# One seven-product chunk in each SwiGLU of a two-layer encoder, the third, with all four of its pairs

## The chip, the cores and the metric

The kernel runs on one core of a Trainium2 chip. The metric is device microseconds of one execution of the whole program. The page of the profile tells of one profiled execution; its engines are PE (matrix products), DVE (element-wise work on two tensors), ACT (copies, Silu, Exp), POOL, and SP, which issues nearly all of the DMAs.

## The reference

Two layers work on 256 rows (tokens) of 1024 numbers, all in float32. Each layer adds half a SwiGLU, then a mixer, then half a SwiGLU:

```python
def swiglu(h, w_gate, w_up, w_down):
    return (jax.nn.silu(h @ w_gate) * (h @ w_up)) @ w_down

for layer in range(DEPTH):
    x = x + 0.5 * swiglu(rms_norm(x, ffn1_norm[layer]), ...)
    x = x + mixer(rms_norm(x, mix_norm[layer]))      # attention; even and odd layers differ
    x = x + 0.5 * swiglu(rms_norm(x, ffn2_norm[layer]), ...)
return rms_norm(x, final_norm)
```

`w_gate` and `w_up` are 1024 x 2816, `w_down` is 2816 x 1024. The mixers are not touched by the change.

## The kernel before

**Stages.** The program is six stages, numbered `now.n`: SwiGLU 0, mixer 1, SwiGLU 2, SwiGLU 3, mixer 4, SwiGLU 5. All weights are read once from HBM, mostly 1 MB at a time, into three buffers called `raw`.

**One product.** Each float32 number is split into a high and a low part, and each product of a 128-row block of activations with a piece of weights of 128 x 512 is three matmuls (`mm`, L469 to L471: high by high, high by low, low by high). "Product" below means these three. For the weights, ACT copies the high part (`hi`, L477) and DVE subtracts it for the low part (`lo`, L480). A `Split` is one such step, of 1024 columns (two pieces) or 512 (one); seven tiles of the kind "wp" hold its results. With every product the function `tick` lets one step of the other tasks be recorded, and new splits are recorded at the rate of the tables `RATE`, `AHEAD_RATE`, `SEVEN_RATE`, if a tile is free (`room`). The order of recording is the order on each engine: every engine's queue is in order, written out by hand.

**A SwiGLU.** The 2816 columns of gate and up are worked off as five chunks of 512 (chunk 0 to 4) and a last one of 256. In a plain chunk two row tiles (`tt` 0 and 1) times eight blocks of the contraction make 16 products for the gate and 16 for up. ACT then takes Silu of the gate (L670), DVE multiplies it with up out of PSUM (`glu`, L675), and the result is turned over by two ACT copies (L554, L558) with a DMA transpose between. The down projection takes 11 pairs of 128-row blocks.

**Seven products for eight.** A pair of contraction blocks of two row tiles, gate and up, is a 2 x 2 by 2 x 2 product, and can be had with seven products (Strassen's scheme in Winograd's form). The table `SEVEN` says which chunks do it and for how many of their four pairs; `DOWN` says it for the down projection, by `s` for seven products and `p` for the plain eight. It costs sums: `strassen` makes from one raw tile the sum `two` and two sums in place (`b12`, `b11`, both in `raw`), and four splits, one of 512 columns and three of 1024. The last two are of the kind "sum" and have three tiles of their own (`shi`, `slo`). `x_sums` makes four sums of the activations (K) ahead of the chunk; `SEVEN_WAIT` and `SEVEN_GAP` say after how many products it starts and how far apart its steps stand. At the end of a chunk of seven, `copy` (ACT, L765), `common`, `first_gate` and `rest` (DVE, L773 to L814) put the seven sums together.

**PSUM.** There are eight banks of 512 columns: two called `pj`, three `s`, one `o`, two `tp`. A plain chunk has its gates in `s` and its ups in `pj`. A chunk of seven has the product sums "00", "01", "10" in `s`, "1" and "5" in `pj`, "7" in `tp`. If one or more of its pairs are plain, these come first and need "11" in `o` too, and "6" lies in `tp`; without a plain pair "6" lies in `o`. After the last plain pair, the chunk waits in the program for the tasks of the chunk before (`finish`), and "1" and "5" take the two `pj` banks over. The plain chunk after a chunk of seven has its first gate in `pj` again, by the table `tags`.

Of the kernel before, what the change touches and what calls it, by code (L numbers as in the profile page):

```python
# [20 lines left out]
NT = 2  # L21
# [12 lines left out]


DOWN = {
# [4 lines left out]
}  # L41

SILUS = {0: 3, 2: 3, 3: 3, 5: 3}
# [39 lines left out]

SEVEN = {
    0: {2: 3},
    2: {1: 3, 3: 2},
    3: {1: 2, 3: 2},
    5: {2: 3},  # L90
}
AHEAD_RATE = {
    0: 0.81,
    2: 0.62,
# [6 lines left out]
    3: 1.2,  # L101
    5: 1.08,
}
SEVEN_WAIT = {
    0: 22,
    2: 4,
    3: 5,
    5: 6,
}
SEVEN_GAP = {  # L110
    0: 2,
    2: 4,
# [93 lines left out]
class Trunk:  # L206
# [88 lines left out]
    def plan(self):  # L295
# [16 lines left out]
        def ffn(n, l, stage):  # L312
            c0 = 0
            for ci, w in enumerate(FF_CHUNKS):
                first = stage == 0 and c0 == 0
                if ci in SEVEN[stage]:
                    for k in range(0, KD, 2):
                        pieces = []
                        for i, name in enumerate(("_w_gate", "_w_up")):
                            src = a[n + name][l][k * P : (k + 2) * P, c0 : c0 + w].rearrange("(k p) n -> p k n", p=P)  # L320
                            pieces.append(((slice(0, P), slice(0, 2), slice(i * w, i * w + w)), src))
                        yield pieces, 2, D, [2], "strassen" if k >= KD - 2 * SEVEN[stage][ci] else "wide"
                    c0 += w
# [28 lines left out]
        def odd():  # L352
# [4 lines left out]
            for g in range(2):  # L357
                for nh in range(2):
                    src = w_out[g * 512 : g * 512 + 512, nh * 512 : nh * 512 + 512].rearrange("(j p) n -> p j n", p=P)
                    yield [(slice(0, P), src)], 4, 512, [2], "narrow"  # L360

        yield from ffn("ffn1", 0, 0)
        yield from even()
        yield from ffn("ffn2", 0, 2)
        yield from ffn("ffn1", 1, 3)
        yield from odd()
        yield from ffn("ffn2", 1, 5)
# [24 lines left out]
    def strassen(self, raw, halves):  # L392


        add = lambda o, x, y: self.nc.vector.tensor_tensor(o, x, y, op=ALU.add)  # L395
        first, second = halves(raw[:, 0, :]), halves(raw[:, 1, :])
        b21, b22, b11, b12 = (t[:, i, :] for t in (first, second) for i in range(2))
        flat = raw.rearrange("p k n -> p (k n)")

        def all_sums():  # L400
            two = splits[2].raw = self.t([P, 2, 512], "two")
            add(two, second[:, 1:2, :].to_broadcast([P, 2, 512]), halves(flat[:, 512:1536]))
            add(b12, two[:, 1, :], b22)
            add(b11, b12, b21)


        splits = [
            Split(second[:, 0:1, :], [1], then=all_sums),
            Split(first, [1]),
            Split(first, [1], kind="sum"),  # L410
            Split(second, [1], True, kind="sum"),
        ]
        return splits
# [243 lines left out]
    def ffn(self):  # L657
# [10 lines left out]
        def silu(tt, w, g, s):  # L668
            yield 1
            nc.scalar.activation(s[:, :w], g[:, :w], AF.Silu, scale=self.rstd_of(tt))  # L670

        def glu(tt, f0, w, u, s):
            yield 1
            m = self.t([P, 512], "glu", 3)
            nc.vector.scalar_tensor_tensor(m[:, :w], u[:, :w], self.now.r[tt], s[:, :w], op0=ALU.mult, op1=ALU.mult)  # L675
            self.spawn(transposed(tt, f0, w, m), GLU_WAIT)
# [44 lines left out]
        K = []  # L721
        sevens = SEVEN[self.now.n]
        most = max(sevens.values())

        def x_sums():

            yield SEVEN_WAIT[self.now.n]
            gap = SEVEN_GAP[self.now.n]
            X = []
            for tt in range(NT):  # L730
                while len(self.now.hT[tt]) < KD:
                    yield 1
                x = self.t([P, 2, 512], ("shi", "slo")[tt], FIT["sum"], F32R).bitcast(F32)
                X.append(x.rearrange("p a (k t) -> p (a k) t", t=P)[:, : 2 * most, :])
                hi, lo = (t.bitcast(F32)[:, KD - 2 * most :, :] for t in self.hts[self.now.n, tt])
                nc.vector.tensor_tensor(X[tt], hi, lo, op=ALU.add)
                yield gap
            k0, k1, k2, k3 = (X[tt][:, i::2, :] for tt in range(NT) for i in range(2))
            for o, x, y, op in [
                (k2, k3, k2, ALU.subtract), (k3, k3, k1, ALU.subtract), (k1, k2, k1, ALU.subtract), (k0, k1, k0, ALU.add)  # L740
            ]:
                nc.vector.tensor_tensor(o, x, y, op=op)
                yield gap

            places = [(f"g0_{sum(FF_CHUNKS[:ci]) // P}_", FF_CHUNKS[ci] // P) for ci in range(max(sevens), len(FF_CHUNKS))]
            places += [(f"k{f}", 4) for f in sorted(paired, reverse=True)]
            for (tag, n), k in zip(places, (k0, k1, k2, k3)):
                hi, lo = (self.t([P, n, P], tag + p, 1, F32R)[:, :most, :] for p in "hl")
                self.high_part(hi, k)
                yield gap  # L750
                self.low_part(lo, k, hi)
                K.append([(hi[:, q, :], lo[:, q, :]) for q in range(most)])

        def seven_gates(f0, w, pairs7):

# [96 lines left out]

        f0 = 0
        self.spawn(x_sums())
        for ci, w in enumerate(FF_CHUNKS):
            if ci in sevens:
                seven_gates(f0, w, sevens[ci])
                f0 += w // P
                continue
            self.rate = (AHEAD_RATE if ci + 1 in sevens else RATE)[self.now.n]  # L860

            tags = ["pj", "s", "s", "pj"] if ci - 1 in sevens else ["s", "s", "pj", "pj"]
            G = self.take(KD)
            S = []
            if self.now.n + ci == 0:
                both = self.first_gates(G)
            for tt in range(NT):
                g = both[tt] if self.now.n + ci == 0 else self.project(self.ready(tt), G, tags[tt])
                S.append(self.t([P, 512], "silu", SILUS[self.now.n]))
                self.start(silu(tt, w, g, S[tt]))  # L870
            U = self.take(KD)
            for tt in range(NT):
                u = self.project(self.now.hT[tt], U, tags[NT + tt])
                tasks.append(self.start(glu(tt, f0, w, u, S[tt])))
            f0 += w // P

        w, V = FF_MIXED, self.take(KD)
        for tt in range(NT):
            both = self.project(self.now.hT[tt], V, "s")
            s = self.t([P, 512], "silu", SILUS[self.now.n])  # L880
# [686 lines left out]
```

## Time and profile before

| what | value |
|---|---|
| median of 3 runs | 942.53 us (942.22 to 944.11) |
| the profiled execution | 944.79 us, of which 943.0 us are its span |
| PE busy | 922.9 us, 98% |
| DVE busy | 788.4 us, 84% |
| ACT busy | 679.1 us, 72% |
| POOL busy | 91.6 us, 10% |
| DMA | 183.16 MB, mean 194 GB/s |
| chain that ended last | PE 66%, DVE 16%, ACT 7%, DMA 5% |

Read it so: PE is hardly ever idle, so its waits are few and can be listed one by one. The busy share of PE counts the modelled, overlapping lives of matmuls; the time from one start to the next tells the real pace. A wait is put down to the instruction that ended it. In the rows of a view by stretch, (x..) counts instructions and PEclk is the granted share of the TensorE clock.

### The profile page before, as it was taken

To read this page: it belongs to the slowest core of one execution; us is meant where nothing else is said; L and a number is where in the kernel's file an instruction comes from. 1 tells how busy PE (TensorE), PEld (TensorE's weight loads), DVE (VectorE), ACT (ScalarE), POOL (GpSimd) and SP (SyncE) were. 2 spreads that over 40 slices of the span, in tenths; PEclk is the share of its full clock that TensorE was granted. 3 is DMA by queue.
4 is the path that set the end of the run, shared out by engine and by line. 5 is a ranking of instruction groups with operands and counts; after the bars stand their busy time and mean duration, and the time that the engine had idled before them with its cause. 6 is when DMAs were issued, how large, how long until landed. Compare 5 with 4: busy or idle time off the path is not lost.

```text
span 943.0 us, 12407 instructions
## 1 busy us (share of the span) xinstructions
PE 922.9 (98%) x4399; PEld 753.5 (80%) x4399; DVE 788.4 (84%) x1228; ACT 679.1 (72%) x1091; POOL 91.6 (10%) x152
## 2 busy tenths in 40 slices
PE   8999999999999999999999999999999999999997
PEld 6887888877778788888888878778878788878886
DVE  6799679778869988888978887989777787988897
ACT  7687876477787777875657778657877577769753
POOL 1300000064410000000100000008030000000001
PEclk9999999999999999999999999999999999999999
DMA  8867875554326687776466777575433458488661
GB/s 286 276 183 245 250 212 213 185 151 100 108 91 200 220 215 227 234 231 236 151 181 224 197 232 229 195 257 171 146 125 134 134 167 257 126 271 254 185 223 45
DMA packets 129344, 183.16 MB, mean 194 GB/s; under 512 B 50689, under 2 KB 63745, under 8 KB 129281
## 3 DMA queue, kind: packets, MB, share of 16 engines
q1 hardware_dynamic: 128704, 181.58, 61.4%
q10 hardware_dynamic: 576, 0.79, 0.2%
q8 instruction: 34, 0.56, 0.2%
q14 instruction: 30, 0.24, 0.1%
HBM read 169.76 MB, written 1.05 MB: 181 GB/s over the span
## 4 chain that ended last, share of the span: by engine, by line
PE 66%; DVE 16%; ACT 7%; DMA 5%; issue 4%; SPq 0%; POOL 0%; POOLq 0%; ACTq 0%; DVEq 0%
PE s L470 9%; PE s L471 9%; PE s L469 9%; PE pj L469 9%; PE pj L470 9%; PE pj L471 9%; DVE lo L480 7%; ACT hi L477 2%; DMA glu<-turned 2%; PE o L1039 2%; DVE raw L395 1%; DVE two L395 1%; PE tp L1118 1%; PE o L469 1%; PE o L470 1%
## 5 line engine op out<-in xcount | busy, mean ns | idle before, releaser
L480 DVE TENSOR_TENSOR lo<-raw,hi 128x1024 fp32r<-128x1024 f32 (+1 forms) x372 | 375.5, 1029 | 80.9 <-ACT hi L477 79.5
L477 ACT ACTIVATE hi<-raw 128x1024 fp32r<-128x1024 f32 (+1 forms) x372 | 319.6, 889 | 57.1 <-PE pj L471 16.5
L470 PE MATMUL s<-lo,th 128*128 128x512 f32 x373 | 145.6, 390 | 2.5 <-DVE lo L480 2.5
L469 PE MATMUL pj<-hi,th 128*128 128x512 f32 x367 | 146.6, 400 | 1.3 <-ACT glu L765 1.3
L469 PE MATMUL s<-hi,th 128*128 128x512 f32 x373 | 146.2, 392 | 0.4 <-ACT hi L477 0.4
L471 PE MATMUL s<-hi,tl 128*128 128x512 f32 x373 | 145.4, 390 | 0.0
L470 PE MATMUL pj<-lo,th 128*128 128x512 f32 x367 | 143.5, 391 | 1.7 <-DVE lo L480 1.6
L471 PE MATMUL pj<-hi,tl 128*128 128x512 f32 x367 | 143.3, 390 | 0.0
L470 PEld LDWEIGHTS s<-lo,th 128*128 128x128 f32 x373 | 70.0, 188 | 18.2 <-DVE lo L480 4.0
L469 PEld LDWEIGHTS s<-hi,th 128*128 128x128 f32 x373 | 70.0, 188 | 14.9 <-ACT hi L477 0.6
L470 PEld LDWEIGHTS pj<-lo,th 128*128 128x128 f32 x367 | 69.1, 188 | 16.0 <-DVE lo L480 3.3
L471 PEld LDWEIGHTS s<-hi,tl 128*128 128x128 f32 x373 | 70.0, 188 | 14.5
L469 PEld LDWEIGHTS pj<-hi,th 128*128 128x128 f32 x367 | 69.0, 188 | 15.6 <-ACT glu L765 1.7
L471 PEld LDWEIGHTS pj<-hi,tl 128*128 128x128 f32 x367 | 68.9, 188 | 14.6
L489 POOL TENSOR_TENSOR rstd<-var,mhalf 128x1 f32<-128x1 f32 (+2 forms) x16 | 17.1, 1070 | 597.5 <-DVE var L487 454.9
L554 ACT COPY turned<-glu 128x1024 uint16<-128x1024 uint16 (+1 forms) x48 | 46.4, 966 | 27.3 <-DVE glu L792 18.9
L558 ACT COPY turned<-glu 128x1024 uint16<-128x1024 uint16 (+1 forms) x48 | 60.1, 1252 | 7.4 <-DMA glu<-turned 7.4
L469 PE MATMUL s<-hi,g_h 128*128 128x512 f32 (+1 forms) x131 | 51.4, 392 | 0.0
L471 PE MATMUL s<-hi,g_l 128*128 128x512 f32 (+1 forms) x131 | 51.0, 389 | 0.0
L470 PE MATMUL s<-lo,g_h 128*128 128x512 f32 (+1 forms) x131 | 50.8, 388 | 0.0
L477 ACT ACTIVATE shi<-two 128x1024 fp32r<-128x1024 f32 x30 | 31.7, 1057 | 26.2 <-DVE two L395 26.1
L477 ACT ACTIVATE shi<-raw 128x1024 fp32r<-128x1024 f32 x30 | 31.7, 1056 | 24.4 <-PE s L471 13.1
(483 smaller groups left out, 1683.1 us busy)
## 6 DMA issues: line engine op xcount, KB each, us to landing
raw<-in_ffn_w_down SPq DMA_DIRECT2D x44, 1024.0 KB, 5.2
raw<-in_ffn_w_up SPq DMA_DIRECT2D x28, 1024.0 KB, 5.2
raw<-in_ffn_w_gate SPq DMA_DIRECT2D x26, 1024.0 KB, 5.2
raw<-in_ffn_w_gate SPq DMA_DIRECT2D x35, 512.0 KB, 3.9
raw<-in_ffn_w_up SPq DMA_DIRECT2D x32, 512.0 KB, 5.0
raw<-in_odd_w_qkv SPq DMA_DIRECT2D x12, 1024.0 KB, 5.3
raw<-in_even_w_in SPq DMA_DIRECT2D x4, 1024.0 KB, 5.1
raw<-in_even_w_out SPq DMA_DIRECT2D x8, 512.0 KB, 5.7
```

The source lines that it names most:

```text
L395: add = lambda o, x, y: self.nc.vector.tensor_tensor(o, x, y, op=ALU.add)
L469: mm(ps, h, wh, start=first, stop=False)
L470: mm(ps, h, wl, start=False, stop=False)
L471: mm(ps, l, wh, start=False, stop=last)
L477: self.nc.scalar.activation(hi, src, AF.Copy)
L480: self.nc.vector.tensor_tensor(lo, src, hi.bitcast(F32), op=ALU.subtract)
L489: nc.gpsimd.tensor_tensor(r[:, :n], v[:, :n], self.mhalf[:, :n], op=ALU.pow)
L554: self.nc.scalar.copy(planes.rearrange("p (h c) -> p h c", h=2), back.rearrange("p (c h) -> p h c", h=2))
L558: self.nc.scalar.copy(planes.rearrange("p (c h) -> p h c", h=2), back.rearrange("p (h c) -> p h c", h=2))
L1039: self.nc.tensor.matmul(O[64 * s : 64 * s + 64, i * P : i * P + P], v(b0 + i, s, kc), pT[s][:, i, kc, :], start=(kc == 0), stop=(kc == 1),)
L1118: nc.tensor.transpose(tb[:, o : o + P], p[:, i, kc * P : kc * P + P], self.ident)
```

## The change

Each SwiGLU has one chunk of seven, chunk 2, with all four pairs (before: chunk 2 with three in SwiGLU 0 and 5; chunk 1 with three and chunk 3 with two in SwiGLU 2; chunks 1 and 3 with two each in SwiGLU 3). One down pair in SwiGLU 0 and one in SwiGLU 5 goes from seven products to eight. The first gate of the next chunk goes into the `tp` bank that the chunk of seven leaves unused. `all_sums` is cut in two: `two` after the first split, the two sums in place after the second. `x_sums` counts its two tiles as taken from the three of the kind "sum" while it works.

```diff
-    0: "p0 p1 p2 s3 p4 s5 p6 s7 p8 p10 p9",
+    0: "p0 p1 p2 p3 p4 s5 p6 s7 p8 p10 p9",
...
-    5: "p3 p0 s2 s5 p4 s1 p9 s7 s8 p6 p10",
+    5: "p3 p0 p2 s5 p4 s1 p9 s7 s8 p6 p10",
...
-SEVEN = {
-    0: {2: 3},
-    2: {1: 3, 3: 2},
-    3: {1: 2, 3: 2},
-    5: {2: 3},
-}
+SEVEN = {0: {2: 4}, 2: {2: 4}, 3: {2: 4}, 5: {2: 4}}
...
-SEVEN_WAIT = {
-    0: 22,
-    2: 4,
-    3: 5,
-    5: 6,
-}
+SEVEN_WAIT = {0: 22, 2: 22, 3: 22, 5: 6}
...
-        def all_sums():
+        def two_sums():
             two = splits[2].raw = self.t([P, 2, 512], "two")
             add(two, second[:, 1:2, :].to_broadcast([P, 2, 512]), halves(flat[:, 512:1536]))
-            add(b12, two[:, 1, :], b22)
+
+        def other_sums():
+            add(b12, splits[2].raw[:, 1, :], b22)
             add(b11, b12, b21)
 
         splits = [
-            Split(second[:, 0:1, :], [1], then=all_sums),
-            Split(first, [1]),
+            Split(second[:, 0:1, :], [1], then=two_sums),
+            Split(first, [1], then=other_sums),
...
                 x = self.t([P, 2, 512], ("shi", "slo")[tt], FIT["sum"], F32R).bitcast(F32)
+                self.live["sum"] += 1
...
                 K.append([(hi[:, q, :], lo[:, q, :]) for q in range(most)])
+            self.live["sum"] -= NT
...
-            tags = ["pj", "s", "s", "pj"] if ci - 1 in sevens else ["s", "s", "pj", "pj"]
+            tags = ["tp", "s", "s", "pj"] if ci - 1 in sevens else ["s", "s", "pj", "pj"]
```

In the changed kernel the lines stand eight to ten higher: L461 to L463 there are L469 to L471 before, L472 is L480, L385 is L395, L667 is L675.

Where instructions stand is shown at three places. The first is DVE in SwiGLU 0, from the middle of chunk 1 to the `glu` of its second row tile, which is row 70 of DVE's queue in both. `raw_429`, `raw_468` and `raw_503` are the raw tiles of the first, second and third pair of chunk 2; `lo` and `slo` are low parts of their splits. Before:

```order
L395 TENSOR_TENSOR raw_468<-raw_468 128x512
L675 SCALAR_TENSOR_TENSOR glu_574<-pj_521,rstd_213,silu_472 128x512
L480 TENSOR_TENSOR g_0_l_572<-turned_459,g_0_h_571 128x512
L480 TENSOR_TENSOR lo_581<-raw_468,hi_580 128x1024
L480 TENSOR_TENSOR slo_588<-two_550,shi_587 128x1024
L480 TENSOR_TENSOR slo_598<-raw_468,shi_597 128x1024
L480 TENSOR_TENSOR lo_607<-raw_503,hi_606 128x512
L395 TENSOR_TENSOR two_613<-raw_503 128x1024
L395 TENSOR_TENSOR raw_503<-two_613,raw_503 128x512
L395 TENSOR_TENSOR raw_503<-raw_503 128x512
L675 SCALAR_TENSOR_TENSOR glu_630<-pj_567,rstd_258,silu_520 128x512
```

And DVE at the same rows (60 to 70) in the changed kernel:

```order
L472 TENSOR_TENSOR slo_545<-two_516,shi_544 128x1024
L472 TENSOR_TENSOR slo_555<-raw_429,shi_554 128x1024
L472 TENSOR_TENSOR lo_565<-raw_468,hi_564 128x512
L385 TENSOR_TENSOR two_571<-raw_468 128x1024
L667 SCALAR_TENSOR_TENSOR glu_584<-pj_526,rstd_213,silu_472 128x512
L472 TENSOR_TENSOR g_0_l_582<-turned_459,g_0_h_581 128x512
L472 TENSOR_TENSOR lo_591<-raw_468,hi_590 128x1024
L385 TENSOR_TENSOR raw_468<-two_571,raw_468 128x512
L385 TENSOR_TENSOR raw_468<-raw_468 128x512
L472 TENSOR_TENSOR slo_600<-two_571,shi_599 128x1024
L667 SCALAR_TENSOR_TENSOR glu_624<-pj_577,rstd_258,silu_525 128x512
```

As many rows stand ahead of the second `glu`; the first pair of chunk 2 is now one with sums, and the two sums in place stand behind the low part of the second split.

The second place is PE at the end of chunk 1 and the start of chunk 2 of SwiGLU 0 (rows 216 to 224). Before:

```order
L469 MATMUL pj_567<-hi_496,th_124 128x512
L470 MATMUL pj_567<-lo_497,th_124 128x512
L471 MATMUL pj_567<-hi_496,tl_125 128x512
L469 MATMUL s_623<-hi_512,th_120 128x512
L470 MATMUL s_623<-lo_513,th_120 128x512
L471 MATMUL s_623<-hi_512,tl_121 128x512
L469 MATMUL s_625<-hi_512,th_124 128x512
```

And PE at the same rows in the changed kernel:

```order
L461 MATMUL pj_577<-hi_496,th_124 128x512
L462 MATMUL pj_577<-lo_497,th_124 128x512
L463 MATMUL pj_577<-hi_496,tl_125 128x512
L461 MATMUL pj_626<-hi_509,th_120 128x512
L462 MATMUL pj_626<-lo_510,th_120 128x512
L463 MATMUL pj_626<-hi_509,tl_121 128x512
L461 MATMUL s_621<-hi_522,th_120 128x512
```

Before, eight plain products lie between the last up and the first that needs a `pj` bank again (row 243, sum "1"; the other `pj` bank, "5", comes four products later). Now "1" comes at once, and "5" is the fifth product of the chunk.

The third place is PE in SwiGLU 3 where a plain chunk follows a chunk of seven. Before, from chunk 3 to chunk 4 (`hi_5268` is the first weight piece of the next gate):

```order
L469 MATMUL tp_5237<-shi_5259,g_16_h_4699 128x512
L470 MATMUL tp_5237<-slo_5260,g_16_h_4699 128x512
L471 MATMUL tp_5237<-shi_5259,g_16_l_4700 128x512
L469 MATMUL pj_5337<-hi_5268,th_4476 128x512
L470 MATMUL pj_5337<-lo_5269,th_4476 128x512
```

And PE in the changed kernel, from chunk 2 to chunk 3 of SwiGLU 3:

```order
L461 MATMUL o_4912<-shi_5024,g_12_h_4733 128x512
L462 MATMUL o_4912<-slo_5025,g_12_h_4733 128x512
L463 MATMUL o_4912<-shi_5024,g_12_l_4734 128x512
L461 MATMUL tp_5101<-hi_5033,th_4436 128x512
L462 MATMUL tp_5101<-lo_5034,th_4436 128x512
```

The last of the seven sums is now in `o`, and the next gate begins in a `tp` bank that nobody holds, not in the `pj` bank of sum "1".

## The prediction

> **What bounds the kernel.** I read the page's busy times first, then PE's waits, then the stretches of the chunks that the change touches, then DVE's timeline there.
>
> ```profile
> span 943.0 us, 12407 instructions
> PE 922.9 (98%) x4399; PEld 753.5 (80%) x4399; DVE 788.4 (84%) x1228; ACT 679.1 (72%) x1091; POOL 91.6 (10%) x152
> ```
>
> PE is busy all but 20 us, so the time is the number of products, times their pace, plus what PE waits. These are PE's longer waits (total us, times, longest):
>
> ```profile
> PE s L470 <- DVE lo L480: 2.5, 3, 2.0
> PE pj L470 <- DVE lo L480: 1.6, 2, 0.9
> PE tp L525 <- DVE x L612: 1.4, 1, 1.4
> PE pj L469 <- ACT glu L765: 1.3, 1, 1.3
> PE s L470 <- DVE slo L480: 1.0, 2, 0.8
> ```
>
> They add up to 7.8 us, all behind DVE but one, and but for 0.2 us at the start all in the SwiGLUs: 0.7 and 0.9 in SwiGLU 0 and 5 (`pj` L470, just behind chunk 2), 2.0 in SwiGLU 2, and 4.0 in SwiGLU 3: the rows of 1.4, 1.3 and 1.0 above come again in its answer for 522 to 640 us, and this one:
>
> ```profile
> PE s L470 <- DVE lo L480: 0.3, 1, 0.3
> ```
>
> PE's timeline gives the pace, and what follows the longest wait:
>
> ```profile
> 53.07 0.39 PE L469 MATMUL s<-hi,th 128*128 128x512 f32 x1
> ...
> 58.51 0.39 PE L469 MATMUL pj<-hi,th 128*128 128x512 f32 x1
> ...
> 61.27 0.50 PE L469 MATMUL pj<-shi,g_h 128*128 128x512 f32 x1
> ...
> 318.26 0.50 PE L470 MATMUL s<-lo,th 128*128 128x512 f32 x1 [1.96 <-DVE lo L480]
> ...
> 319.61 0.63 PE L469 MATMUL tp<-shi,k14h 128*128 128x512 f32 x1
> 320.03 0.63 PE L470 MATMUL tp<-slo,k14h 128*128 128x512 f32 x1
> ```
>
> From 53.07 to 58.51 stand eight products, so one takes 0.68 us. After the wait of 1.96 us matmuls start 0.42 us apart, not 0.23. The stretches show the clock there, and how full DVE is:
>
> ```profile
> core 0: us, PE busy (x) PEld busy (x) DVE busy (x) ACT busy (x) POOL busy (x), PEclk, DMA share, GB/s
> 53.10:73.20 20.10, 20.10 (x89) 16.10 (x88) 19.96 (x23) 16.06 (x20) 0.00 (x0) 1.00 0.48 137
> 73.20:96.00 22.80, 22.07 (x97) 17.91 (x96) 21.31 (x27) 17.67 (x22) 0.00 (x0) 1.00 0.86 278
> 318.00:323.00 5.00, 4.74 (x14) 3.78 (x15) 5.00 (x6) 4.50 (x6) 0.00 (x0) 0.66 0.31 84
> 522.60:545.50 22.90, 20.90 (x91) 16.60 (x89) 19.36 (x24) 18.41 (x25) 0.00 (x0) 1.00 0.61 165
> 578.90:639.60 60.70, 58.98 (x262) 47.88 (x261) 55.18 (x74) 39.59 (x61) 0.13 (x1) 1.00 0.59 202
> 803.90:823.80 19.90, 19.90 (x88) 16.16 (x87) 17.99 (x21) 14.90 (x19) 0.00 (x0) 1.00 0.49 134
> 823.80:846.80 23.00, 22.15 (x98) 17.95 (x97) 21.40 (x27) 15.60 (x19) 0.00 (x0) 1.00 0.81 262
> ```
>
> The first row is chunk 2 of SwiGLU 0: DVE is busy 19.96 of 20.10 us, and so is it for most of the next chunk (21.31 of 22.80); SwiGLU 5 looks alike (17.99 of 19.90, then 21.40 of 23.00). The clock of 0.66 over 5 us cost some 1.7 us more in SwiGLU 2. So the waits that the change can reach are 0.7 + (2.0 + 1.7) + 4.0 + 0.9 = 9.3 us.
>
> **The change, part by part.**
>
> *Products.* Chunks of seven save one product a pair: 3, 5, 4 and 3 pairs before, four in each now. The down projection saves 3, 3, 4 and 5 before, 2, 3, 4 and 4 now. By SwiGLU that is 0, +1, 0 and 0: one product more, +0.7 us, on the path, since PE is the bound.
>
> *DVE's work.* This is its queue around the start of chunk 2 in SwiGLU 0, and the ACT copy that it waits for first:
>
> ```profile
> 43.15 1.06 ACT L477 ACTIVATE hi<-raw 128x1024 fp32r<-128x1024 f32 x1 [3.62 <-DMA raw<-in_ffn_w_up]
> 44.12 1.34 ACT L558 COPY turned<-glu 128x1024 uint16<-128x1024 uint16 x1
> 44.24 1.24 DVE L480 TENSOR_TENSOR lo<-raw,hi 128x1024 fp32r<-128x1024 f32 x1 [2.75 <-ACT hi L477]
> 47.68 1.23 DVE L480 TENSOR_TENSOR lo<-raw,hi 128x1024 fp32r<-128x1024 f32 x1 [2.19 <-ACT hi L477]
> 48.82 0.68 DVE L480 TENSOR_TENSOR g_l<-turned,g_h 128x512 fp32r<-128x512 f32 x1
> 49.42 0.69 DVE L480 TENSOR_TENSOR lo<-raw,hi 128x512 fp32r<-128x512 f32 x1
> 50.03 1.22 DVE L395 TENSOR_TENSOR two<-raw 128x1024 f32<-128x1024 f32 x1
> 51.28 0.69 DVE L395 TENSOR_TENSOR raw<-two,raw 128x512 f32<-128x512 f32 x1
> 52.00 0.69 DVE L395 TENSOR_TENSOR raw<-raw 128x512 f32<-128x512 f32 x1
> 52.61 0.74 DVE L675 SCALAR_TENSOR_TENSOR glu<-pj,rstd,silu 128x512 f32<-128x512 f32 x1
> 53.27 0.68 DVE L480 TENSOR_TENSOR g_l<-turned,g_h 128x512 fp32r<-128x512 f32 x1
> ...
> 60.47 0.74 DVE L675 SCALAR_TENSOR_TENSOR glu<-pj,rstd,silu 128x512 f32<-128x512 f32 x1
> ```
>
> From start to start: 1.14 us for a low part of 1024 columns, 0.60 for one of 512, 1.25 for `two`, 0.72 and 0.61 for the sums in place, 0.66 for `glu`. A seven-product pair costs DVE 0.60 + 1.25 + 0.72 + 0.61 + 3 x 1.14 = 6.6 us and PE 7 x 0.68 = 4.8; a plain pair 2.3 and 5.4. One such pair fewer in all, and two chunk ends fewer (SwiGLU 2 and 3, some six operations of 0.6 us each more than a plain chunk's two), against four wider `x_sums`: DVE loses some 10 us of its 788. That pays only where PE waits for DVE. What counts is where the work stands: four pairs in a row are 26.4 us on DVE beside 28 x 0.68 = 19.0 on PE.
>
> *The start of chunk 2.* The second `glu` is row 70 on DVE before and after. The 16 rows ahead of it from row 54 add up to 13.9 us in both. Before, it ran at 60.47 to 61.21, 7.4 us after the last up (53.07), and nobody waited: "5" came as the thirteenth product, at 61.27, just in time. Now "1" is the first product and "5" the fifth. The first raw tile of chunk 2 lands at 43.1 as before (that queue is not touched), and DVE begins at 43.8, after ACT's copy of 512 columns. ACT's turning copy (1.34 us) keeps the second split back 0.4 us; the 2.19 us before is gone. So the first `glu` ends at 53.9: "1" waits 0.8 us. The second ends near 43.8 + 13.9 + 0.4 + 0.7 = 58.8: "5", due at 53.9 + 4 x 0.68 = 56.6, waits 2.2. Sum 3.0 us in SwiGLU 0. For the other three I need one more row of DVE and two of the page, ACT's:
>
> ```profile
> 790.28 2.58 DVE L480 TENSOR_TENSOR lo<-raw,hi 128x1024 fp32r<-128x1024 f32 x2 [3.39 <-ACT hi L477]
> ...
> L554 ACT COPY turned<-glu 128x1024 uint16<-128x1024 uint16 (+1 forms) x48 | 46.4, 966 | 27.3 <-DVE glu L792 18.9
> L477 ACT ACTIVATE shi<-raw 128x1024 fp32r<-128x1024 f32 x30 | 31.7, 1056 | 24.4 <-PE s L471 13.1
> ```
>
> In SwiGLU 5 DVE has caught up at 790.3; from there to the end of the second `glu` stand six low parts of 1024, two of 512, two `two`, two pairs of sums in place, two `glu` and 1.9 us of turned results, in all 16.4: 806.7, 2.8 after the last up (803.9, where the stretch of chunk 2 begins) against 2.7 needed: 0.1. In SwiGLU 3 ACT has a turning copy and a copy of a sum to do over the last two products (1.0 + 1.0 against 1.4, so 0.6 left), then DVE a low part and the `glu` (1.14 + 0.66): 2.4, nothing. In SwiGLU 2 `x_sums` is spread by gaps of 4 products over the whole of chunk 1, now holds two of the three sum tiles, and so keeps the second sum of the first pair back until the chunk starts. Behind the same 0.6 of ACT two low parts, `two` and `glu` then stand in a row (1.14 + 0.60 + 1.25 + 0.66): 4.3 us, so 1.6 of waiting at "5".
>
> *The end of chunk 2.* Sum tiles bound how far DVE can run ahead: the fourth sum is free to be made when "5" of the first pair is done, 5 x 0.68 = 3.4 us in. From there ACT's copy (1.0), one low part (1.1), the third pair (6.6) and the fourth up to its first sum (0.60 + 1.25 + 1.14 + 1.33 + 1.14 = 5.5) end at 17.6 us. PE needs this at its 25th product, its second matmul, 16.5 us in: 1.1 late. The next low parts and the two of the next chunk's gate, with the turned results and `first_gate` between, cost 0.4 more. So 1.5 us in each SwiGLU, where three pairs behind a plain one showed 0.7 and 0.9. A wait at the start shifts both sides alike. In SwiGLU 2 DVE has the held-back pair to do as well: 20.5 us against 16.5, so 4.0 + 0.4 = 4.4, the 1.6 at "5" in it.
>
> *The free bank.* It removes the 1.3 us wait for `copy` in SwiGLU 3, the only place where it showed. *The two lots* bring the second split's low part forward by 1.33 us in each such pair; products "00" and "01" need it. That is worth something only where these are the late ones, and at the end of the chunk the sums are: nothing.
>
> *SwiGLU 3.* Its 4.0 us go with the chunk of seven at place 3: DVE and ACT, behind by its end, carried this into the down projection (55.18 us of DVE in 60.70). Now a whole plain chunk lies between. I put 1.5 in its place.
>
> Sum of waits: 3.0 + 1.5 in SwiGLU 0, 4.4, 1.5, and 1.5 + 0.1 in SwiGLU 5: 12.0 against 9.3, so +2.7, and with the product +3.4 us. The profiled execution (944.79 us, 1.8 around its span) would go to 948.2; it is 2.3 above the median, so against 942.53 I predict 945.9. The ends of the terms: the start of chunk 2 in SwiGLU 0 between nothing (DVE just in time, as before) and 3.0; the ends of the chunks between nothing and twice 1.5.
>
> *The clock.* By the rows above, a wait of 1.96 us was followed by a clock of 0.66 over 5 us; the waits of 1.4 and 1.3 us in SwiGLU 3 by no such dip (its rows show 1.00). A wait of 2.2 us at "5" would so cost 1.7 more: 947.6. [...]
>
> **Rivals.** *The chunk's DVE work stays hidden* (the other side). If PE doesn't wait at the ends of the four chunks, because the two lots and the earlier sums keep DVE ahead, 4 x 1.5 = 6.0 go: 939.9. For it: DVE does 10 us less, and three pairs cost only 0.7 to 0.9. Against: 26.4 us beside 19.0, with three sum tiles. It ends faster than before only from 5.3 us of these 6.0 on. *The second glu is in time* in SwiGLU 0: minus 3.0, 942.9, no change. For it: DVE stood idle 2.75 and 2.19 us there before; against: the same 13.9 us stand ahead of it. *The dip*: 947.6. *The gain in SwiGLU 3 doesn't come*, since its down order still holds three seven-product pairs close together: of its old waits behind place 3 (1.4, 0.3, and 0.2 of the 1.0) stay, +1.9: 947.8.
>
> **Chances.** My forecast 0.33 (its own range 944.5 to 947.2), the dip 0.14, SwiGLU 3 0.10, the `glu` in time 0.28, DVE hidden 0.15. A measurement here can tell about 0.2% (1.9 us) from no change. So slower by more 0.57, within it 0.28, faster 0.15. The range 940.6 to 948.6 leaves out about 1 in 10 on either side.
>
> **What would show it.** In SwiGLU 0 PE waits for `glu` (DVE, L667) at `pj`, twice, up to 2 us; near the end of each chunk 2 it waits for `slo` by about 1 us; in SwiGLU 3 no waits for `x` or `copy`. I am wrong if PE's waits in the four SwiGLUs come to less than 9 us.

## The result, and the profile after

The changed kernel takes 950.62 us (median of 6 runs, 950.09 to 951.02), the kernel before 942.50 beside it (6 runs, 941.92 to 944.11): a ratio of 1.0079, 95% interval 1.0068 to 1.0089. It is 8.1 us slower, where 3.4 were forecast, and 950.62 lies above the range. The direction was right, and so were most of the places; the price of a wait, SwiGLU 5 and the base of the sum were not.

The profiled execution of the changed kernel took 950.09 us. Its span and busy times:

```profile
span 947.9 us, 12362 instructions
PE 925.4 (98%) x4402; PEld 752.4 (79%) x4402; DVE 777.6 (82%) x1195; ACT 677.0 (71%) x1081; POOL 99.1 (10%) x152
```

PE has three matmuls (one product) more and DVE 10.8 us less to do, as the forecast had it (some 10). PE's longer waits (total us, times, longest):

```profile
PE tp L462 <- DVE slo L472: 4.0, 5, 0.8
PE pj L461 <- DVE glu L667: 2.8, 2, 1.8
PE s L462 <- DVE lo L472: 2.1, 6, 0.5
...
PE tp L462 <- DVE lo L472: 0.7, 3, 0.2
```

That is 9.6 us in 16 waits, where the rows shown of before hold 7.8 in nine. Some 2 us of idle time more do not make 8. PE's timeline at the end of chunk 2 in SwiGLU 0 shows what it leaves out (start, duration, and in brackets the idle time):

```profile
71.44 0.39 PE L463 MATMUL s<-hi,g_l 128*128 128x512 f32 x1
71.67 0.40 PE L461 MATMUL tp<-shi,k14h 128*128 128x512 f32 x1
72.87 0.50 PE L462 MATMUL tp<-slo,k14h 128*128 128x512 f32 x1 [0.81 <-DVE slo L472]
73.21 0.40 PE L463 MATMUL tp<-shi,k14l 128*128 128x512 f32 x1
73.45 0.40 PE L461 MATMUL pj<-shi,g_h 128*128 128x512 f32 x1
```

A matmul that waits for nothing starts 0.23 us after the one ahead. Here it is 1.20, and 0.34 for the next: 0.97 + 0.11 = 1.08 us lost, where the list has 0.81. The matmul ahead counts as busy until 0.40 us behind its start, so 0.16 us of every wait lie under it, and the matmul behind a wait takes 0.11 longer. Each wait costs its idle time and 0.27 us, and a short one isn't listed at all: at 74.60 one of 0.06 us, without a bracket in the trace, cost 0.33. Summed from start to start, PE loses 5.0 us in SwiGLU 0 (its start apart, where both kernels wait), 4.3 in 2, 2.9 in 3 and 4.3 in 5. In before it lost 1.2, 2.6, 5.6 and 1.2, the dip of the clock in SwiGLU 2 apart.

This table goes by stage: microseconds from a SwiGLU's first product to the next stage's first (for SwiGLU 5 to the end of PE's last matmul), in each profile. An asterisk marks a stage in which PE's granted clock fell behind a wait, to 0.50 for 3.4 us (a dip).

| kernel | SwiGLU 0 | SwiGLU 2 | SwiGLU 3 | SwiGLU 5 |
|---|---|---|---|---|
| before, first profile | 180.5 | 180.3* | 181.9 | 177.3 |
| before_again | 179.7 | 178.9 | 184.4* | 177.3 |
| changed | 183.6 | 181.2 | 179.2 | 180.3 |
| after_again | 184.5 | 181.3 | 179.5 | 180.3 |
| only05 | 184.3 | 178.8 | 181.9 | 180.5 |
| only2 | 179.8 | 181.3 | 182.6 | 177.3 |
| only3 | 179.8 | 180.3* | 179.2 | 177.3 |
| five_tp | 182.5 | 181.2 | 179.2 | 179.0 |
| old_bank | 185.7* | 181.2 | 179.1 | 180.3 |
| no_lots | 183.8 | 180.7 | 179.8 | 179.9 |
| pool_sums | 192.4* | 187.8* | 190.1 | 185.1 |
| sums_out | 181.2 | 177.0 | 176.6 | 176.2 |
| sum4 | 182.8* | 183.4* | 179.4 | 181.0 |
| down_only | 180.0 | 178.7 | 185.0* | 177.1 |
| three | 180.2 | 177.9 | 177.7 | 177.3 |
| three_down | 180.2 | 177.9 | 177.8 | 177.1 |

Stages with the same code agree within 0.4 us, but for the dips and three places: the start of SwiGLU 0 in the first profile of before (a wait for `x`, 0.7 more), a wait for the first `glu` at "1" in SwiGLU 0 that one profile of the changed kernel has and the other lacks (0.9), and in SwiGLU 3 of before a wait for `x` that was 1.4 to 2.8 us long.

### The profile page after: what moved, and what is told of

The parts are those of the page before. It is cut to its first block, busy times and chain, and to the rows that moved or that the text cites. A ratio compares the mean times of both kernels' runs of the same rounds, so it can differ in the third digit from the quotient of the medians.

```text
span 947.9 us, 12362 instructions
## 1 busy us (share of the span) xinstructions
PE 925.4 (98%) x4402; PEld 752.4 (79%) x4402; DVE 777.6 (82%) x1195; ACT 677.0 (71%) x1081; POOL 99.1 (10%) x152
## 4 chain that ended last, share of the span: by engine, by line
PE 75%; DVE 13%; ACT 7%; issue 3%; DMA 0%; POOL 0%; POOLq 0%; ACTq 0%; DVEq 0%
PE s L462 11%; PE s L463 11%; PE s L461 11%; PE pj L461 10%; PE pj L463 10%; PE pj L462 10%; DVE lo L472 5%; ACT hi L469 2%; ACT shi L469 2%; PE o L462 2%; PE o L463 2%; PE o L461 2%; PE o L1033 2%; DVE raw L385 2%; DVE two L385 1%
## 5 line engine op out<-in xcount | busy, mean ns | idle before, releaser
L472 DVE TENSOR_TENSOR lo<-raw,hi 128x1024 fp32r<-128x1024 f32 (+1 forms) x372 | 377.0, 1031 | 85.9 <-ACT hi L469 83.5
L469 ACT ACTIVATE hi<-raw 128x1024 fp32r<-128x1024 f32 (+1 forms) x372 | 320.1, 891 | 62.6 <-PE s L463 25.4
L461 PE MATMUL pj<-hi,th 128*128 128x512 f32 x368 | 146.9, 399 | 0.0
L463 PE MATMUL pj<-hi,tl 128*128 128x512 f32 x368 | 143.6, 390 | 0.0
L462 PE MATMUL s<-lo,th 128*128 128x512 f32 x352 | 137.8, 391 | 2.1 <-DVE lo L472 2.1
L461 PE MATMUL s<-hi,th 128*128 128x512 f32 x352 | 138.0, 392 | 0.1
L463 PE MATMUL s<-hi,tl 128*128 128x512 f32 x352 | 137.2, 390 | 0.0
L463 PEld LDWEIGHTS pj<-hi,tl 128*128 128x128 f32 x368 | 69.1, 188 | 14.7
L462 PEld LDWEIGHTS s<-lo,th 128*128 128x128 f32 x352 | 66.1, 188 | 18.2 <-DVE lo L472 4.9
L461 PEld LDWEIGHTS pj<-hi,th 128*128 128x128 f32 x368 | 69.2, 188 | 14.0 <-issue 0.9
L461 PEld LDWEIGHTS s<-hi,th 128*128 128x128 f32 x352 | 66.1, 188 | 13.9 <-ACT hi L469 0.4
L463 PEld LDWEIGHTS s<-hi,tl 128*128 128x128 f32 x352 | 66.1, 188 | 13.6
L469 ACT ACTIVATE shi<-raw 128x1024 fp32r<-128x1024 f32 x29 | 30.7, 1060 | 53.5 <-PE s L463 25.3
L461 PE MATMUL s<-hi,g_h 128*128 128x512 f32 (+1 forms) x140 | 54.9, 392 | 0.0
L463 PE MATMUL s<-hi,g_l 128*128 128x512 f32 (+1 forms) x140 | 54.4, 388 | 0.0
L462 PE MATMUL s<-lo,g_h 128*128 128x512 f32 (+1 forms) x140 | 54.3, 388 | 0.0
L472 DVE TENSOR_TENSOR slo<-raw,shi 128x1024 fp32r<-128x1024 f32 x29 | 35.5, 1223 | 19.0 <-ACT shi L469 18.5
```

The lines of the kernel that those rows point to most:

```text
L461: mm(ps, h, wh, start=first, stop=False)
L462: mm(ps, h, wl, start=False, stop=False)
L463: mm(ps, l, wh, start=False, stop=last)
L469: self.nc.scalar.activation(hi, src, AF.Copy)
L472: self.nc.vector.tensor_tensor(lo, src, hi.bitcast(F32), op=ALU.subtract)
```

## The experiments

### One stage at a time, and before once more

Each round of runs has its own runs of before beside it. Their medians lay between 942.5 and 944.6 us, so kernels of different rounds are best compared by their ratios to before or by stage.

The change was made in some SwiGLUs alone, all parts of it together; the others keep the tables and the order of before. The edit of only3:

```diff
+SEVEN = {0: {2: 3}, 2: {1: 3, 3: 2}, 3: {2: 4}, 5: {2: 3}}
+NEW = {3}
...
+            if self.now.n not in NEW:
+                other_sums()
...
+            tags = ["tp" if self.now.n in NEW else "pj", "s", "s", "pj"] if ci - 1 in sevens else ["s", "s", "pj", "pj"]
```

> The kernel before, unchanged, profiled a second time. Theory A (the first profile of before was of an untypical execution: after PE's wait of 1.96 us in SwiGLU 2 the clock stood at 0.66 for 5 us, and most executions have no such dip): the span is 940.2 to 941.0 us, and the stretch of 5 us behind that wait shows a clock of 1.00 or the wait is shorter; then only some 0.7 + 2.0 + 4.0 + 0.9 us of waits were to be had, and the forecast should have been taken from the sum with the 1.7 us of the dip put back. Theory B (the dip belongs to every execution, and the 2.3 us between profile and median are spread over the whole program): the dip is there again, 0.6 to 0.7 over 5 us, whatever the span.

> The change in SwiGLU 0 and 5 alone, SwiGLU 2 and 3 as before. Theory A (the loss arises in SwiGLU 0 and 5, where the plain pair ahead of the three pairs of seven is gone, so that PE waits for the second glu at the fifth product and for low parts near the chunk's end; each wait costs its idle time and some 0.27 us beside it): 6.1 us slower than before (3.1 in SwiGLU 0, 3.0 in SwiGLU 5), about 948.6. The forecast's own terms: 3.8 + 0.7 = 4.5 slower, about 947.0. Theory C (the loss against the median is in SwiGLU 2, hidden in the profile by the dip of the clock there): at most 3 us slower.

> The change in SwiGLU 2 alone. Theory A (most executions of before have no dip of the clock in SwiGLU 2, so the comparison of the two profiles, which gives +0.95 us there, is 1.7 to 2.7 too low): 2.7 to 3.6 us slower, 945.2 to 946.1. Theory B (the dip is in every execution of before): 0.95 slower, 943.5. The forecast's terms: 1.4 slower with the dip counted among the waits removed, 3.1 without.

> The change in SwiGLU 3 alone: chunk 2 with four pairs in place of chunks 1 and 3 with two each, the free bank and the two lots there. Theory A (its old waits behind place 3, 4.0 us, go, and waits of 1.5 us come at the end of chunk 2): 2.7 us faster than before by the stages of the two profiles, 939.8; the forecast's term was 2.5. Rival (the gain comes only with less work left over from the stages ahead): nothing to 1 us faster. The sum of the three one-stage kernels' differences should give the whole change's 8.1 us if the stages do not act on each other.

Measured beside a median of before of 943.91: only05 951.96 (ratio 1.0093, 1.0078 to 1.0109), only2 945.3 (1.0024, 1.0013 to 1.0035), only3 940.84 (0.997, 0.996 to 0.998). In medians +8.0 + 1.4 - 3.1 = +6.4 (of the unrounded), where the whole change has 7.6 to 8.1. By stage they add up: the four changed stages sum to 725.2 us here, against 724.3 and 725.5 in the two profiles of the changed kernel. The loss is mostly in SwiGLU 0 and 5, and SwiGLU 3's gain of 2.7 us came in full. By stage only05 costs 4.5 + 3.3, more than the 6.1 expected of it: the first profile of before, from which these 6.1 came, had 0.8 too much in SwiGLU 0, and this run has 0.35 us of waiting at "1" that the changed kernel's first profile lacks.

before_again decides the base against the forecast. PE's rows at the long wait of SwiGLU 2, and then behind a wait at the end of SwiGLU 3:

```profile
317.48 0.50 PE L470 MATMUL s<-lo,th 128*128 128x512 f32 x1 [1.99 <-DVE lo L480]
317.81 0.39 PE L471 MATMUL s<-hi,tl 128*128 128x512 f32 x1
318.05 0.40 PE L469 MATMUL s<-hi,g_h 128*128 128x512 f32 x1
...
633.28 0.66 PE L525 MATMUL tp<-mats,x 128*128 128x128 f32 x4 [2.28 <-DVE x L612]
...
634.53 0.63 PE L469 MATMUL s<-hi,g_h 128*128 128x512 f32 x1
634.95 0.63 PE L470 MATMUL s<-lo,g_h 128*128 128x512 f32 x1
```

The same wait, here 1.99 us, and no dip: SwiGLU 2 takes 178.9 us, 1.4 less than in the first profile. The dip came elsewhere this time, behind 2.28 us. Theory A's reason was right, its span (940.2 to 941.0) was not: 943.9, because of the wait and the dip in SwiGLU 3. only2 cost 1.4 us in medians and 2.4 by stage against an undisturbed SwiGLU 2, short of the 2.7 that A set: before holds the dip in some executions, and then only2 takes it away.

### One part undone each

```diff
 # five_tp: "5" in the free bank, the next gate in pj
-[("1", "pj"), ("5", "pj"), ("7", "tp")]
+[("1", "pj"), ("5", "tp"), ("7", "tp")]
-tags = ["tp", "s", "s", "pj"]
+tags = ["pj", "s", "s", "pj"]
 # old_bank: the second of these lines alone
 # no_lots
+                other_sums()          # again behind two
-            Split(first, [1], then=other_sums),
+            Split(first, [1]),
 # pool_sums: the two sums in place on POOL
-            add(b12, splits[2].raw[:, 1, :], b22)
-            add(b11, b12, b21)
+            pool_add(b12, splits[2].raw[:, 1, :], b22)
+            pool_add(b11, b12, b21)
```

> The changed kernel, with sum "5" in the free tp bank and the next chunk's first gate in pj again (in the bank that the second glu left long ago), so that the fifth product of chunk 2 no longer needs the second glu. Theory A (in SwiGLU 0 and 5 PE waits for that glu alone, and each wait costs its listed idle time and some 0.27 us more: 1.94 + 0.11 and 1.13 + 0.11 in the profile): both waits go and do not come back; stage 0 181.6, stage 5 179.1, the whole 3.3 us faster than the changed kernel, about 947.3. Rival (DVE is late there by as much anyhow, and the wait moves to low parts at the chunk's end): less than 1 us faster.

> The changed kernel, with the next chunk's first gate in the pj bank of sum "1" as before. If the free bank matters in this kernel, PE waits for ACT's copy of "1" at the start of chunk 3 as it did in SwiGLU 3 before (1.27 us and 0.27 about it); the forecast saw that wait in SwiGLU 3 alone: 1.5 us slower than the changed kernel, 952.1. Rival (PE is held by DVE at the end of chunk 2 anyhow, so ACT's copy is done in time): no change, and the free bank was worth nothing.

> The changed kernel, with the sums made in one lot again, behind the first split. The forecast gave the two lots nothing, since the sums are the late ones: 0 +- 0.5 us for the whole, 950.1 to 951.1, with the waits at each chunk's end moved but not changed in sum. Rival (the second split, needed by the products 00 and 01, is what PE waits for at s, 0.4 us in each chunk 2): 4 x 1.3 = 5 us slower.

> The changed kernel, with the two sums in place of each seven-product pair on POOL instead of DVE, everywhere. Theory A (the waits at the end of each chunk 2 are DVE's rate: 6.6 us a pair beside PE's 4.8; without the two sums 5.3 a pair, so over the third and fourth pair DVE is 2.7 us earlier): the waits for slo and lo behind the third pair, 2.9 to 4.3 us in each SwiGLU with their restarts, 13 in all, fall to a third or less; 8 to 11 us faster than the changed kernel, 940 to 943. Theory B (the three sum tiles set the pace): the waits stay, less than 2 us faster. Rival C (a sum takes some 1.5 us on POOL, by its row of 128x512, and DVE's operations beside it grow): the fourth split is late instead, 0 to 5 us faster, and DVE's rows of 1.22 and 0.69 us get longer.

*five_tp*: 947.96 (before beside it 944.11; ratio 1.0039, 1.0029 to 1.005), 2.7 us under the changed kernel's first median and 2.4 faster by stage. SwiGLU 5 gains 1.3: its wait for `glu` is gone and nothing took its place. SwiGLU 0 gains 1.1 of 2.0, since this profile has 0.58 us (0.74 lost) of waiting for the first `glu`, at "1", which the changed kernel's first profile lacks and after_again has. So the plain pair ahead had been the cover for the two `glu`, and for the second of them a free bank does the same without a product more.

*old_bank*: 951.38 (1.0072, 1.005 to 1.0095). The expected 1.5 us did not come; the stages are those of the changed kernel within 0.1 us, but for SwiGLU 0, where this profile has a wait at "1" of 0.94 us and a dip. In each of the four, PE does wait for ACT's copy:

```profile
PE pj L461 <- ACT glu L759: 1.8, 4, 0.4
```

and then not for the low parts that it met there before. DVE held PE at that place anyhow, and the free bank was worth nothing.

*no_lots*: 951.32 (1.007, 1.0048 to 1.0093); the four stages sum to 724.2 us against 724.3. The waits move, from the end of the chunk to its start and to one low part. In the sum nothing is gained or lost, as forecast; by stage it is between 0.6 less and 0.7 more, so these cancel rather than vanish.

```profile
PE s L463 <- DVE lo L473: 6.9, 6, 1.5
PE pj L462 <- DVE glu L668: 4.8, 5, 1.8
```

*pool_sums*: 980.07 (1.0372, 1.0345 to 1.04), 29 us slower than the changed kernel where A had 8 to 11 faster. The rows (mean ns behind the comma), first POOL's, then DVE's, and behind them one place in POOL's timeline and in DVE's:

```profile
L386 POOL TENSOR_TENSOR raw<-two,raw 128x512 f32<-128x512 f32 x29 | 60.5, 2087 | 482.8 <-DVE two L385 309.2 <-ACT hi L470 137.4 <-DMA glu<-turned 27.4
L386 POOL TENSOR_TENSOR raw<-raw 128x512 f32<-128x512 f32 x29 | 53.0, 1828 | 2.3
...
L473 DVE TENSOR_TENSOR slo<-two,shi 128x1024 fp32r<-128x1024 f32 x29 | 51.8, 1787 | 6.0 <-ACT shi L470 5.6
```

```profile
67.42 2.20 POOL L386 TENSOR_TENSOR raw<-two,raw 128x512 f32<-128x512 f32 x1 [8.45 <-DVE two L385]
```

```profile
68.53 2.18 DVE L473 TENSOR_TENSOR slo<-two,shi 128x1024 fp32r<-128x1024 f32 x1
72.97 1.23 DVE L473 TENSOR_TENSOR slo<-raw,shi 128x1024 fp32r<-128x1024 f32 x1 [2.27 <-ACT shi L470]
```

Two sums take 3.9 us on POOL, not the 3.0 that I took from its nearest row, against 1.3 on DVE, and the low part beside them takes 1.79 instead of 1.22. The fourth split is late by that, and DVE stands still for 2.27 us. Rival C, far worse than its own number. In the place shown DVE's low part starts at 68.53, beside POOL's first sum (67.42 to 69.62), and takes 2.18 us; why it takes longer, the run doesn't show.

### DVE's rate or the sum tiles

sums_out leaves the sums b12 and b11 out; sum4 has another tile for sums and one fewer for the plain splits.

```diff
 # sums_out
-            add(b12, splits[2].raw[:, 1, :], b22)
-            add(b11, b12, b21)
 # sum4
-FIT = {"wp": 7, "sum": 3}
+FIT = {"wp": 6, "sum": 4}
```

> The changed kernel with the two sums in place of every seven-product pair left out (1.33 us of DVE a pair, gate and up and down alike; the fourth split then takes the raw values, which costs no time), so that DVE has 5.3 us a pair and nothing stands in their place. Theory A (the end of chunk 2 is DVE's rate): DVE is 2.7 us earlier over the third and fourth pair, and the five waits behind the third pair, 2.9 us with their restarts in SwiGLU 0, 3.0 in 5, 2.8 in 3 and 4.3 in 2, fall to 0.5 or less each, also the glu wait at the fifth product in SwiGLU 0 and 5 by 1.3: span 947.9 down to 933 to 937. Theory B (the three sum tiles set it: the fourth sum waits for the end of the first pair's "5", whatever DVE has to do): DVE's idle time of 2.15 us behind that tile grows and the waits at the end fall by less than half: span 940 to 945.

> The changed kernel with four tiles for sums and six for plain splits (before: three and seven), the same memory. Theory B (the tiles): DVE's idle time of 2.15 us ahead of the fourth low part of a sum goes, DVE stands some 2 us earlier for the rest of chunk 2, and the waits behind the third pair fall from 2.9 us to 1 or less in each SwiGLU. Theory A (DVE's rate alone): DVE's queue is full anyhow and the waits stay within 0.5 us. Plain chunks may lose by the seventh tile; the chunk of seven is read by itself.

*sums_out*: a span of 934.2 us, 13.7 under the changed kernel's, in theory A's range. At the end of no chunk 2 is a wait listed any more, and the wait for `glu` fell to 0.46 us in SwiGLU 0 and to nothing in 5. *sum4*: DVE's timelines in SwiGLU 0 at the fourth sum's low part (the second of the second pair's two), in the changed kernel, sum4, five_tp and sums_out:

```profile
59.29 1.23 DVE L472 TENSOR_TENSOR slo<-raw,shi 128x1024 fp32r<-128x1024 f32 x1 [2.15 <-ACT shi L469]
```

```profile
57.88 1.22 DVE L472 TENSOR_TENSOR slo<-raw,shi 128x1024 fp32r<-128x1024 f32 x1
```

```profile
57.93 1.23 DVE L472 TENSOR_TENSOR slo<-raw,shi 128x1024 fp32r<-128x1024 f32 x1
```

```profile
59.44 1.23 DVE L471 TENSOR_TENSOR slo<-raw,shi 128x1024 fp32r<-128x1024 f32 x1 [2.15 <-ACT shi L468]
```

In sum4 the idle time of 2.15 us is gone, and DVE is 1.4 us earlier. What counts is not this idle time but how far DVE stands behind PE's first "5", whose end frees the tile. The row starts 2.1 us behind "5" in the changed kernel (57.19), 2.0 in five_tp (55.95), which has no idle time here and still loses 3.0 us at the chunk's end, and 2.1 in sums_out (57.35), which has the same idle time and no wait at the end. In sum4 it starts 0.1 ahead of "5" (58.02). In the two SwiGLUs where sum4 has no dip it loses 0.5 us more at the chunk's start, and the chunk's end costs PE 1.1 us instead of 2.4 (SwiGLU 3) and 0.1 instead of 3.0 (SwiGLU 5). So it is both, and they add: DVE starts some 2 us late behind the tile, then loses 1.8 us on every pair (6.6 against 4.8). Without the sums all of the wait goes, with a fourth tile more than half. SwiGLU 2 of the changed kernel has no idle time at this row; there DVE comes late by its own queue. Over the whole, sum4 is no cure: 964.49 us, since with six plain tiles mixer 1 takes 5.7 us more and mixer 4, with a dip, 6.7.

### Three pairs, and the down orders

```diff
 # three, from before
+SEVEN = {0: {2: 3}, 2: {2: 3}, 3: {2: 3}, 5: {2: 3}}
+SEVEN_WAIT = {0: 22, 2: 22, 3: 22, 5: 6}
 # down_only, from before; three_down has both
-    0: "p0 p1 p2 s3 p4 s5 p6 s7 p8 p10 p9",
+    0: "p0 p1 p2 p3 p4 s5 p6 s7 p8 p10 p9",
-    5: "p3 p0 s2 s5 p4 s1 p9 s7 s8 p6 p10",
+    5: "p3 p0 p2 s5 p4 s1 p9 s7 s8 p6 p10",
```

> The kernel before with one chunk of seven in every SwiGLU, the third, with three pairs behind a plain one (four in the changed kernel), sums in one lot, old bank, old down orders. Three products more than before (2 in SwiGLU 2, 1 in SwiGLU 3, 0.68 us each: 2.0 us). My reading (the fourth pair in a row is what costs, by the missing cover at the start of the chunk and DVE's lag at its end; three pairs behind a plain one cost 0.9 to 1.0 us as in SwiGLU 0 and 5 of before): SwiGLU 2 about 178.9 us (178.9 before without a dip of the clock), SwiGLU 3 about 178.0 (181.9 before), the others as before: 3.9 us faster than before without its dips, median 938.5 to 939.5, faster than both kernels. Rival (products decide: 3 more than before are 2.0 us slower, and the old waits in SwiGLU 3 come from its down order): 942 to 946.

> The kernel before with the down orders of the changed one alone: one pair fewer of seven in SwiGLU 0 and 5. Theory A (PE is the bound there and waits for nothing): one product of 0.68 us more in each, stage 0 180.4 (179.7 in most profiles of before), stage 5 177.95 (177.27). Rival (a pair of seven costs DVE and ACT enough that its product saved is lost again): no change.

*three*: 938.40 us (937.95 to 939.61), ratio 0.9939, 0.9921 to 0.9957, 6.2 us faster than before, where only3 was faster by 3.1. It has three products more (2.0 us of PE), and still wins 1.0 us in SwiGLU 2, where I expected none, and 4.2 or more in SwiGLU 3. Its waits for low parts:

```profile
PE pj L460 <- DVE lo L470: 1.5, 2, 0.8
...
PE s L460 <- DVE lo L470: 0.7, 2, 0.5
```

*down_only*: 947.41 us in its one run, which holds the long wait for `x` (2.79 us) and a dip. By stage neither theory is right: a product more in each, and +0.2 in SwiGLU 0, -0.2 in 5. The wait near the start of chunk 3 (0.73 and 0.85 us listed in before) is no longer listed there. DVE's rows ahead of that low part in before, and in down_only:

```profile
75.77 0.42 DVE L705 TENSOR_TENSOR quarters<-turned,quarters 128x256 f32<-128x256 f32 x1
76.11 0.55 DVE L480 TENSOR_TENSOR g_l<-turned,g_h 128x384 fp32r<-128x384 f32 x1
76.58 0.28 DVE L712 TENSOR_TENSOR quarters<-quarters 128x128 f32<-128x128 f32 x1
76.89 0.29 DVE L713 TENSOR_TENSOR quarters<-quarters 128x128 f32<-128x128 f32 x1
77.10 2.35 DVE L480 TENSOR_TENSOR lo<-raw,hi 128x1024 fp32r<-128x1024 f32 x2
```

```profile
75.41 0.68 DVE L480 TENSOR_TENSOR g_l<-turned,g_h 128x512 fp32r<-128x512 f32 x1
76.01 1.22 DVE L480 TENSOR_TENSOR lo<-raw,hi 128x1024 fp32r<-128x1024 f32 x1
77.66 1.22 DVE L480 TENSOR_TENSOR lo<-raw,hi 128x1024 fp32r<-128x1024 f32 x1 [0.42 <-ACT hi L477]
```

A down pair of seven has its sums made here (`quarters`), where PE waits for DVE; the product that it saves is lost at this place again. One part of the change was never undone alone: that `x_sums` counts its two tiles.

### What was open

> The changed kernel, unchanged, timed again beside before and profiled a second time. The stages of the profiles that show no dip of the clock give +3.9 (SwiGLU 0), +2.4 (2), -2.7 (3), +3.0 (5): 6.6 us slower, while the first medians differed by 8.1. Theory A (the runs of before vary by their dips and by the wait for x at the end of SwiGLU 3, 942.0 to 947.6, and the first six of them were quick ones; those of the changed kernel hold none of these): before again near 944, the changed kernel again 950 to 951, so 6 to 7 us between them. Theory B (something beside PE's waits in the SwiGLUs costs the changed kernel 1.5 us that a profile does not show): 8 us between them whatever the median of before.

> One chunk of seven with three pairs behind a plain one in every SwiGLU (938.4 us), and the changed kernel's down orders with it: two products more. Theory A (DVE's sums for a down pair of seven, quarters, stand ahead of the low parts that PE waits for at the end of chunk 2, and without them that wait of 0.9 to 1.0 us with its restart goes, as it did with the down orders alone in the kernel before): stage 0 and 5 within 0.3 us of before, 938.0 to 938.9. Rival (a product more is 0.68 us): 939.8.

*after_again*: 951.12 (950.46 to 951.65) against 943.47, ratio 1.0078, 1.0065 to 1.0091: 7.6 us, between the two theories. Its profile has the wait for the first `glu` in SwiGLU 0 (0.61 us listed), so that stage is 0.9 longer than in the first. The means of both profiles against the undisturbed stages of before give +4.3, +2.4, -2.6 and +3.0, in all 7.1. The last store adds 0.6: it ends 4.3 us after its issue in both profiles of the changed kernel, 3.7 in both of before. The time around the span adds 0.35 (2.15 to 2.2 against 1.8). That makes 8.0, against 7.6 and 8.1. Theory A was right that before varies (941.9 to 947.7 over all runs) and theory B that something lies outside of PE's waits: these 0.95 us, whose cause stays open; three, five_tp, only3 and down_only have the late store too (4.3 to 4.6 us), only05 and only2 do not (3.7 and 3.9).

*three_down*: 938.13 (937.81 to 938.33), ratio 0.9941, 0.9928 to 0.9955: equal to three, as theory A had it, and the rival's 939.8 did not come.

## Why the prediction was wrong

The miss is 4.7 us, 945.9 to 950.62. Two steps make 4.0 of it, and a third term, the price of a wait, was mis-sized in SwiGLU 0, 3 and 5.

*The dip, counted twice: 1.7 us.* "It is 2.3 above the median, so against 942.53 I predict 945.9" took the first profile's excess off the changed kernel too. Of this excess 1.4 was the dip in SwiGLU 2, and the same text counts 1.7 for it among the waits that the change takes away. The other 0.8 was SwiGLU 0, 180.5 us against 179.7 in the second profile; no term counts that, so it was rightly taken off. Without both, the first profile comes to 942.6, the median.

*SwiGLU 5, 2.3 us: forecast +0.7, measured +3.0.* "Six low parts ... in all 16.4: 806.7 ... against 2.7 needed: 0.1" counted DVE's work and none of its waits. SwiGLU 5 starts 1.33 us later in the changed profile, so that end would be 808.0; it was 809.0. DVE's row has the difference:

```profile
798.07 1.23 DVE L472 TENSOR_TENSOR slo<-two,shi 128x1024 fp32r<-128x1024 f32 x1 [1.03 <-ACT shi L469]
```

ACT's turning copy (1.34 us) stood ahead of that `shi`, the step that I did count in SwiGLU 0. So PE waited 0.97 us for the second `glu`, and with the hidden 0.27 that cost 1.2, where 0.1 was forecast. The rest is the end of the chunk: 3.0 us in five waits, forecast 1.5. (Against this, the wait of before that went was worth 1.2, not 0.9.)

*The price of a wait.* The forecast 1.5 us at each end of chunk 2 was about the right idle time (1.6 in SwiGLU 0: 0.41 + 0.81 + 0.06 + 0.23 + 0.09). In five waits it costs 3.0. In SwiGLU 0 this was hidden by a term that fell the other way: 3.0 forecast at its start, 2.1 lost (1.78 listed), because the wait at "1" of 0.8 us was absent from that profile; after_again has it, with 0.77 lost. So +3.8 forecast and +3.8 lost was luck, for both halves were wrong. In SwiGLU 2 the start took no wait at all: +1.4 was forecast, 3.1 without the credit for the dip, and +2.4 came against a profile without one (+0.95 against the first, which has it).

What is left of the 4.7 us: 0.6 in the last store, 0.35 around the span and 0.5 by which the changed kernel's profile lay under its median, less what SwiGLU 2 (against 3.1) and SwiGLU 3 came out lower than forecast, 0.7 + 0.2. That makes 4.6; SwiGLU 0 against 179.7 adds the last 0.1.

The second `glu` of SwiGLU 0, DVE's row and then PE's in the changed kernel:

```profile
56.40 0.74 DVE L667 SCALAR_TENSOR_TENSOR glu<-pj,rstd,silu 128x512 f32<-128x512 f32 x1
```

```profile
57.19 0.50 PE L461 MATMUL pj<-shi,g_h 128*128 128x512 f32 x1 [1.78 <-DVE glu L667]
```

Right were: the count of one product more; `glu` at `pj` as a new wait, up to 2 us, as these rows have it; the wait for `slo` of 0.8 at every end of chunk 2; no wait for `x` or `copy` in SwiGLU 3 in the first profile (0.19 for `x` in the second) and its gain (2.5 forecast, 2.7); nothing for the two lots in the sum. Wrong was what the free bank does: with the old bank the wait for `copy` in SwiGLU 3 is 0.45 us, not 1.3, and stands in the place of waits for low parts, so the bank gains nothing. The rivals "DVE stays hidden" and "the second `glu` in time" did not come, nor did the dip in the changed kernel's own profiles. That the wait at "5" brings no dip, as the sum of 945.9 has it, no row of before had shown: it was my assumption. The changed kernel's wait of 1.78 us was followed by a clock of 1.00, old_bank's of 1.80 by 0.50.

## What to carry to other kernels

Price a wait of PE by start-to-start times, not by the listed idle time: here 0.27 us more each, so that five short waits cost twice what they show. Before a sum is made against one profiled execution, look for what in it happens in some executions only, and never both count it as gained and take it off the base. Saving products pays until the engine that makes their sums falls behind: three pairs behind a plain one (938.4 us) beat four in a row (950.6) with two products more.

## What the runs showed of the hardware

*The clock.* The 0.66 above is a mean over 5 us: in the dip of before the granted clock was 0.50 for 3.41 us, and the 5 us around a dip in only3, old_bank, pool_sums and sum4 have the same mean. In before the clock fell twice, at 319.42 us and, behind PE's last matmul, at 940.65. These times are 621.23 us apart, 182 times 3.413. So I cut each profile into stretches of 3.413 us from a fall of its clock. Here are the last stretch before the dip in before, and the dip; then the two in before_again over which the same wait lay:

```profile
316.00:319.41 3.41, 1.45 (x7) 0.97 (x6) 3.38 (x5) 3.02 (x4) 0.00 (x0) 1.00 0.69 259
319.42:322.83 3.41, 3.41 (x10) 2.66 (x9) 3.41 (x4) 3.08 (x4) 0.00 (x0) 0.50 0.32 72
```

```profile
313.53:316.94 3.41, 1.96 (x9) 1.28 (x7) 3.34 (x5) 1.61 (x2) 0.00 (x0) 1.00 0.81 248
316.94:320.35 3.41, 2.87 (x13) 2.38 (x14) 3.41 (x4) 3.41 (x5) 0.00 (x0) 1.00 0.16 59
```

The clock stands behind the bracket of POOL's, PE's busy time behind the first comma. In before the wait lay in one stretch, which left PE idle for 1.96 of its 3.41 us; in before_again an edge cut the same wait, into 1.45 and 0.54. Over all stretches up to PE's last matmul, the clock of before fell behind the one with 1.96 us of idle time and behind none of the others, which had up to 1.20. This wait of 1.96 to 1.99 us stands in five profiles: in before and only3 the 5 us behind it have a mean clock of 0.66, in before_again, only05 and down_only 1.00. That the place of the edges decides is my estimate from the rows shown. The dip in SwiGLU 2 cost 1.4 us (180.3 against 178.9). In the changed kernel no stretch up to PE's last matmul was followed by a fall; the most idle time in one was 1.78 us, the wait for the second `glu`, and in old_bank 1.80 was followed by a dip:

```profile
53.97:57.38 3.41, 1.63 (x8) 1.05 (x7) 3.14 (x5) 0.00 (x0) 0.00 (x0) 1.00 0.63 99
57.38:60.79 3.41, 3.41 (x16) 2.78 (x16) 1.26 (x2) 2.60 (x4) 0.00 (x0) 1.00 0.00 0
```

```profile
55.51:58.92 3.41, 1.61 (x7) 1.03 (x7) 3.04 (x4) 0.00 (x0) 0.00 (x0) 1.00 0.73 103
58.92:62.33 3.41, 3.41 (x9) 2.68 (x9) 1.13 (x1) 2.22 (x3) 0.00 (x0) 0.50 0.00 0
```

*POOL beside DVE.* A sum of 128x512 took 1.83 and 2.09 us in the mean on POOL in pool_sums, 0.69 on DVE in the changed kernel, and DVE's low part of `two` took 1.79 us in the mean in pool_sums, 1.22 in the changed kernel.
